# A half unit's low part in one VectorE instruction of 1024 columns instead of two of 512

## The chip, the core and the metric

The kernel runs on one core of a Trainium2 chip. The core has a matrix engine, TensorE (PE, with its weight loads shown apart as PEld), and three engines for elementwise work: VectorE (DVE), ScalarE (ACT) and GpSimd (POOL). SyncE (SP) issues most of the DMA transfers from HBM. SBUF is the on-chip memory that the engines read and write, PSUM the memory that matmuls accumulate into. Each engine runs its instructions in one fixed order and waits where an instruction's inputs or buffers aren't ready. The metric is the device time of one execution in microseconds. Three runs of the kernel before gave 2400.18, 2401.51 and 2401.63, a median of 2401.51; the profiled execution, from which all rows below come, took 2397.69.

## The reference

256 rows of width 1024 in float32 go through six layers. The first four are transformer layers (block 1): an attention mixer of one of three kinds, a layer norm, a SwiGLU feed-forward net, a layer norm.

```python
def first_block(x, positions, ln_g, ln_b, ...):
    for i in range(DEPTH):                       # 4
        kind, j = i % N_MIXERS, i // N_MIXERS
        ...                                      # h = mixer_a, mixer_b or mixer_c of x
        x = layer_norm(DN_ALPHA * x + h, ln_g[i, 0], ln_b[i, 0])
        x = layer_norm(DN_ALPHA * x + swiglu(x, w_gate_up[i], w_down[i]), ln_g[i, 1], ln_b[i, 1])
    return x
```

The last two (block 2) project the normed rows with one wide matrix `w_in`, run three branches on the parts (chunked spatial gating, a Mamba-2 state-space mixer, differential attention), gate each branch's projection with a sigmoid, and follow with `w_out` and a feed-forward net with a causal convolution; their norms are RMS norms. Nearly all arithmetic is matmuls of the 256 rows with weight matrices, 381.88 MB of weights and other inputs being read through the hardware DMA queue in one execution.

## The kernel before, in words

**Matmuls of three products.** PE multiplies in a reduced 32-bit format, `fp32r`. To keep float32 accuracy each operand is split in two: a high part, its value rounded to fp32r, and a low part, what the rounding left. `mm3` (L389 to L396) issues three matmuls for each product: rows high x weights high (L394), rows high x weights low (L395), rows low x weights high (L396). A matmul takes 128 rows of the contraction against 512 columns.

**Weights.** `plan` lists all weight units in the order of their use. A unit is loaded as two half units of 128 x 1024 values (two contraction slices of 512 columns for most matrices; one slice of 1024 for those called `rows`; 128 x 64 for the small `dt`). `load` (L367 to L387) makes a half unit ready: a DMA on SP's queue into a buffer `raw` (four of them), the high part `w[:, 0]` by a copy on ACT (L382), and the low part `w[:, 1] = raw - w[:, 0]` by a subtraction (L385). The result is in one of seven buffers `w` (one more in block 1). A buffer `raw` is free for the next DMA when its low part is made. `get` asks for the next half unit one ahead of the one in use (AHEAD = 1), and L394 to L396 wait for the parts that they read. All but 11 of the 728 half units have their low part made on DVE; the 11 in `self.aside` (L1427 to L1431), which follow directly on a change between mixer and feed-forward weights in block 1, on POOL.

**Two row tiles.** The rows are two tiles of 128, t = 0 and 1. Each runs through the layers as its own stream of steps, a Python generator, with tasks of its own (`spawn`, `turn`), and `run` lets the two streams take turns, tile 1 four turns behind (LAG). So while one tile is in a norm, the matmuls of the other can fill PE. The instruction lists that result are ordered once more by a scheduler under the kernel's language, engine by engine, so that independent instructions stand between dependent ones.

**Norms.** `layer_norm` (L521) adds the residual (L526), takes mean and variance (L507, L509), and a reciprocal root by three Newton steps on one column (`rsqrt`: L469, then L473 and L477 three times), and scales the rows (L533, L536). All are DVE instructions, each of which needs the one before. At the end of block 1 the normed rows are multiplied by the next norm's gain (`rms_norm`, L958, `rmsh`) and transposed by PE (L439). In the second block `yt` is a branch output that PE has transposed and ACT (L432) and DVE (L433) split into its parts; `sg` (L1318) is a branch's projection times its gate. `xth`, `xtl`, `fht` and `ho` are parts of split rows, made the same way.

Four further lines of the program set what the prediction speaks of:

```python
BUFS = dict(wr=4, wh=7, wx=1, ...)                     # raw buffers, w buffers
AHEAD = 1
nc.vector.scalar_tensor_tensor(h, h, r, b[:, s], ...)  # L536, needs the third Newton step
e = nc.gpsimd if 2 * i + a in self.aside else nc.vector
```

The functions that the change touches and what calls them:

Of the kernel before, what the change touches and what calls it, by code (L numbers as in the profile page):

```python
# [9 lines left out]
F32 = mybir.dt.float32  # L10
# [72 lines left out]
class Net:  # L83
# [283 lines left out]
    def load(self, i, a):  # L367
        nc = self.nc
        _, (kt, n), parts = self.units[i]
        k = kt // 2  # L370
        raw = self.wr.tile([P, 1024], F32, name="raw")[:, :k * n]
        rv = raw.rearrange("p (k n) -> p k n", n=n)
        for o, m, src in parts:
            nc.sync.dma_start(rv[:, :, o:o + m], src[:, k * a:k * a + k])
        if i == a == 0:
            self.load_x()
        if i < self.units_1 and (2 * i + a) % (BUFS["wh"] + BUFS["wx"]) >= BUFS["wh"]:
            w = self.own("w", [2, 1024], "wx", F32R)
        else:
            w = self.wh.tile([P, 2, 1024], F32R, name="w")  # L380
        m = k * n
        nc.scalar.copy(w[:, 0, :m], raw)  # L382
        e = nc.gpsimd if 2 * i + a in self.aside else nc.vector
        for s in (slice(0, m // 2), slice(m // 2, m)):
            e.tensor_sub(w[:, 1, s], raw[:, s], w[:, 0, s].bitcast(F32))  # L385
        return w[:, :, :k * n].rearrange("p two (k n) -> p two k n", n=n)


# [1096 lines left out]
```

## Time and profile before

| | before |
|---|---|
| median of three runs | 2401.51 us |
| profiled execution | 2397.69 us |
| its span (first to last instruction) | 2395.8 us |
| mean granted clock of PE | 0.999 |
| PE busy | 2358.1 us, 98% |
| DVE busy | 1739.8 us, 73% |
| ACT busy | 1320.2 us, 55% |
| POOL busy | 148.1 us, 6% |
| low parts on DVE (L385) | 942.9 us in 1434 instructions |
| high parts on ACT (L382) | 758.5 us in 728 instructions |

How to read it: busy time is the time in which an engine has an instruction under way, and consecutive records of one engine can overlap a little, since an instruction may start before the one ahead of it has left the engine; so the pace is read from start to start in a timeline, and the sum of records is somewhat above the time they take. A number in square brackets behind a row is idle time of the engine before it, with the instruction that ended it. The trace names a tile without its buffer number.

### The profile page before, as it was taken

How to read it: one execution, taken by the hardware profiler on the slowest of the kernel's cores; microseconds unless marked ns; L12 is line 12 of the kernel's file. 1: busy time of each engine (PE TensorE's matmuls, PEld its weight loads, DVE VectorE, ACT ScalarE, POOL GpSimd, SP SyncE). 2: the span in 40 equal slices, each digit the busy share in tenths (PEclk: the TensorE clock that was granted, in tenths of full speed). 3: DMA queues.
4: the chain of work that ended last, by engine and by line, in shares of the span. 5: the costliest groups of instructions: out<-in, count | busy, mean ns of one | idle time of the engine just before them, and what ended most of it. 6: DMA issues, size and time to landing. Idle time of an engine off the chain costs nothing.

```text
span 2395.8 us, 35093 instructions
## 1 busy us (share of the span) xinstructions
PE 2358.1 (98%) x11720; PEld 1926.0 (80%) x11720; DVE 1739.8 (73%) x4255; ACT 1320.2 (55%) x2182; POOL 148.1 (6%) x428
## 2 busy tenths in 40 slices
PE   8999999999999999999999999999999999999999
PEld 6788878888788788887778878887888788888887
DVE  7755576666755767557775588987877889987876
ACT  6544456555444555444544445744577656545776
POOL 1100000000100001000010000100011201000111
PEclk9999999999999999999999999999999999999999
DMA  6366654444566545665365657567565686575653
GB/s 233 106 189 189 185 167 132 133 132 131 171 189 187 185 132 167 187 188 184 124 182 190 186 140 168 136 147 198 165 194 184 166 187 132 123 213 172 189 184 115
DMA packets 280117, 400.16 MB, mean 167 GB/s; under 512 B 20588, under 2 KB 205098, under 8 KB 279936
## 3 DMA queue, kind: packets, MB, share of 16 engines
q1 hardware_dynamic: 274784, 381.88, 54.8%
q0 software_dynamic: 5152, 16.05, 2.2%
q8 instruction: 92, 1.51, 0.3%
q14 instruction: 89, 0.73, 0.1%
HBM read 396.81 MB, written 1.05 MB: 166 GB/s over the span
## 4 chain that ended last, share of the span: by engine, by line
PE 87%; DVE 8%; DMA 3%; ACT 2%; issue 1%; SPq 0%; ACTq 0%; DVEq 0%
PE pj L394 21%; PE pj L396 21%; PE pj L395 21%; PE tp L439 4%; PE ch L394 4%; PE ch L396 4%; PE ch L395 4%; PE ch L596 3%; PE ch L634 2%; DVE w L385 2%; DMA raw<-in_w_in_dram 2%; PE tp L646 1%; ACT w L382 1%; DMA raw<-in_a_w_qkv_dram 1%; DVE convy L985 1%
## 5 line engine op out<-in xcount | busy, mean ns | idle before, releaser
L385 DVE TENSOR_TENSOR w<-raw,w 128x512 fp32r<-128x512 f32 x1434 | 942.9, 684 | 469.3 <-ACT w L382 468.2
L382 ACT CAST w<-raw 128x1024 fp32r<-128x1024 f32 x728 | 758.5, 1043 | 661.2 <-PE pj L396 370.9
L394 PE MATMUL pj<-w,xth 128*128 128x512 f32 x2048 | 820.4, 401 | 7.1 <-ACT xth L432 6.8
L395 PE MATMUL pj<-w,xth 128*128 128x512 f32 x2048 | 803.3, 393 | 1.1 <-DVE w L385 1.1
L396 PE MATMUL pj<-w,xtl 128*128 128x512 f32 x2048 | 802.4, 393 | 1.8 <-DVE xtl L433 1.8
L394 PEld LDWEIGHTS pj<-w,xth 128*128 128x128 f32 x2048 | 385.5, 188 | 90.8 <-ACT xth L432 12.4
L396 PEld LDWEIGHTS pj<-w,xtl 128*128 128x128 f32 x2048 | 385.0, 188 | 86.4 <-DVE xtl L433 5.0
L395 PEld LDWEIGHTS pj<-w,xth 128*128 128x128 f32 x2048 | 386.0, 188 | 76.8 <-DVE w L385 2.0
L394 PE MATMUL ch<-w,fht 128*128 128x512 f32 x412 | 171.4, 416 | 1.8 <-ACT fht L432 1.8
L396 PE MATMUL ch<-w,fht 128*128 128x512 f32 x412 | 161.4, 392 | 0.0
L395 PE MATMUL ch<-w,fht 128*128 128x512 f32 x412 | 160.9, 391 | 0.0
L985 DVE SCALAR_TENSOR_TENSOR convy<-xc,ffn_cw,convy 128x128 f32<-128x128 f32 x352 | 100.7, 347 | 7.1 <-POOL ffn_hist L976 2.1
L396 PEld LDWEIGHTS ch<-w,fht 128*128 128x128 f32 x412 | 77.3, 188 | 17.9 <-DVE fht L433 1.0
L394 PEld LDWEIGHTS ch<-w,fht 128*128 128x128 f32 x412 | 77.5, 188 | 15.4 <-ACT fht L432 3.9
L395 PEld LDWEIGHTS ch<-w,fht 128*128 128x128 f32 x412 | 77.9, 189 | 11.9
L623 ACT ACTIVATE pexp<-ch,nm 128x128 f32<-128x128 f32 (+1 forms) x192 | 65.6, 421 | 33.8 <-DVE nm L618 24.0
L827 ACT ACTIVATE ffg<-pj 128x256 f32<-128x256 f32 x88 | 33.8, 384 | 86.2 <-PE pj L396 86.2
L982 ACT ACTIVATE convy<-xc,ffn_cw 128x128 f32<-128x128 f32 x176 | 72.8, 484 | 1.4
L634 PEld LDWEIGHTS ch<-v,pt 128*128 128x128 f32 x576 | 70.6, 192 | 2.9
L394 PE MATMUL pj<-w,fht 128*128 128x512 f32 x180 | 71.3, 396 | 0.0
L396 PE MATMUL pj<-w,fht 128*128 128x512 f32 x180 | 70.7, 393 | 0.0
L395 PE MATMUL pj<-w,fht 128*128 128x512 f32 x180 | 70.2, 390 | 0.0
(333 smaller groups left out, 2758.8 us busy)
## 6 DMA issues: line engine op xcount, KB each, us to landing
raw<-in_w_gate_up_dram SPq DMA_DIRECT2D x352, 256.0 KB, 3.2
raw<-in_w_in_dram SPq DMA_DIRECT2D x128, 512.0 KB, 5.1
raw<-in_w_down_dram SPq DMA_DIRECT2D x88, 512.0 KB, 3.6
raw<-in_ffn_w_up_dram SPq DMA_DIRECT2D x176, 256.0 KB, 3.3
raw<-in_b_w_qkv_dram SPq DMA_DIRECT2D x144, 256.0 KB, 3.1
raw<-in_ffn_w_down_dram SPq DMA_DIRECT2D x44, 512.0 KB, 4.4
raw<-in_a_w_qkv_dram SPq DMA_DIRECT2D x24, 512.0 KB, 4.4
raw<-in_c_w_qkv_dram SPq DMA_DIRECT2D x48, 256.0 KB, 3.2
```

Of the source, the lines that this page charges most:

```text
L382: nc.scalar.copy(w[:, 0, :m], raw)
L385: e.tensor_sub(w[:, 1, s], raw[:, s], w[:, 0, s].bitcast(F32))
L394: mm(ps, xh[:, k, :], wh[:, kk, cols], start=start, stop=False)
L395: mm(ps, xh[:, k, :], wl[:, kk, cols], start=False, stop=False)
L396: mm(ps, xl[:, k, :], wh[:, kk, cols], start=False, stop=stop)
L439: self.nc.tensor.transpose(tp[:, b * P:(b + 1) * P], src[:, b * P:(b + 1) * P], self.ident)
L596: nc.tensor.matmul(svs[par][:, a, j * P:(j + 1) * P], q(par, a), k(par, a, j), start=True, stop=True)
L623: nc.scalar.activation(p[:, a, :(t + 1) * P], sv[:, a, :], AF.Exp, bias=n2[:, a:a + 1])
L634: nc.tensor.matmul(o[:, par + 2 * a, :], pts[par][:, a * (t + 1) + j, :], v(j, par + 2 * a), start=j == 0, stop=j == t)
L827: nc.scalar.activation(g, ps[:, :FFC], AF.Silu)
L982: nc.scalar.activation(y[:, a, :], xc[:, a, 4:], AF.Identity, bias=b[:, 0, c:c + 1], scale=w[:, h, c:c + 1])
L985: nc.vector.scalar_tensor_tensor(y[:, a, :], xc[:, a, o:o + P], w[:, j, c:c + 1], y[:, a, :], op0=OP.mult, op1=OP.add)
```

## The change

The loop over two halves of the columns at the end of `load` is replaced by one subtraction over all of them. High part, buffers, DMAs and matmuls are the same. On the engines that is one instruction where there were two, at DVE 717 for 1434, on POOL 11 for 22. Lines after it move up by one (L385 becomes L384, L433 becomes L432, L958 becomes L957).

```diff
         m = k * n
         nc.scalar.copy(w[:, 0, :m], raw)
         e = nc.gpsimd if 2 * i + a in self.aside else nc.vector
-        for s in (slice(0, m // 2), slice(m // 2, m)):
-            e.tensor_sub(w[:, 1, s], raw[:, s], w[:, 0, s].bitcast(F32))
+        e.tensor_sub(w[:, 1, :m], raw, w[:, 0, :m].bitcast(F32))
         return w[:, :, :k * n].rearrange("p two (k n) -> p two k n", n=n)
```

With fewer instructions the scheduler also places others differently. Two places show it. A number behind a tile's name is that of its buffer's allocation; they are counted anew in the changed program, so the same half unit has another number there.

DVE at the end of block 1 before (1402.6 to 1408 us in the trace): the last layer norm of row tile 0 (`x_93`, `rs_y_13266`), with the half units 13442 and 13464 and row tile 1's residual (`x_120`) between its steps.

```order
L477 SCALAR_TENSOR_TENSOR rs_y_13266<-rs_a_13267,rs_y_13266 128x1
L385 TENSOR_TENSOR w_13442<-raw_13440,w_13442 128x512
L473 SCALAR_TENSOR_TENSOR rs_a_13267<-rs_y_13266,bnve_13264 128x1
L385 TENSOR_TENSOR w_13464<-raw_13462,w_13464 128x512
L477 SCALAR_TENSOR_TENSOR rs_y_13266<-rs_a_13267,rs_y_13266 128x1
L526 SCALAR_TENSOR_TENSOR x_120<-x_120,ch_12083 128x512
L473 SCALAR_TENSOR_TENSOR rs_a_13267<-rs_y_13266,bnve_13264 128x1
L526 SCALAR_TENSOR_TENSOR x_120<-x_120,pj_12084 128x512
L477 SCALAR_TENSOR_TENSOR rs_y_13266<-rs_a_13267,rs_y_13266 128x1
L385 TENSOR_TENSOR w_13464<-raw_13462,w_13464 128x512
L536 SCALAR_TENSOR_TENSOR x_93<-x_93,rs_y_13266,lnb_13219 128x512 x2
L958 TENSOR_TENSOR rmsh_13281<-x_93,ng_13279 128x512
```

A fourth half, the first of 13442, stands eight instructions ahead of the second, behind the norm's L509. The same place in the changed program, where 13442 and 13464 are 13023 and 13044, and the two half units after them 13058 and 13093:

```order
L476 SCALAR_TENSOR_TENSOR rs_y_12849<-rs_a_12850,rs_y_12849 128x1
L384 TENSOR_TENSOR w_13044<-raw_13042,w_13044 128x1024
L472 SCALAR_TENSOR_TENSOR rs_a_12850<-rs_y_12849,bnve_12847 128x1
L525 SCALAR_TENSOR_TENSOR x_120<-x_120,ch_11719 128x512
L476 SCALAR_TENSOR_TENSOR rs_y_12849<-rs_a_12850,rs_y_12849 128x1
L525 SCALAR_TENSOR_TENSOR x_120<-x_120,pj_11720 128x512
L472 SCALAR_TENSOR_TENSOR rs_a_12850<-rs_y_12849,bnve_12847 128x1
L384 TENSOR_TENSOR w_13058<-raw_13056,w_13058 128x1024
L476 SCALAR_TENSOR_TENSOR rs_y_12849<-rs_a_12850,rs_y_12849 128x1
L384 TENSOR_TENSOR w_13093<-raw_13091,w_13093 128x1024
L535 SCALAR_TENSOR_TENSOR x_93<-x_93,rs_y_12849,lnb_12804 128x512 x2
L957 TENSOR_TENSOR rmsh_12864<-x_93,ng_12862 128x512
```

Here too a fourth low part, 13023, stands eight instructions ahead of 13044, behind the norm's L508. The chain's own steps and the two L526 are the same; in place of four halves of two half units there are four whole half units.

DVE in the state-space stretch of the first block-2 layer before (1637 to 1646.7 us in the trace), with the splits of `yt`, the low parts of the half units 15717 to 15788, and the gated projection `sg`:

```order
L385 TENSOR_TENSOR w_15717<-raw_15715,w_15717 128x512
L477 SCALAR_TENSOR_TENSOR rssm1_13505<-rs_a_15631,rssm1_13505 128x1
L433 TENSOR_TENSOR yt_15707<-tp_15708,yt_15707 128x512
L385 TENSOR_TENSOR w_15746<-raw_15744,w_15746 128x512 x2
L385 TENSOR_TENSOR w_15764<-raw_15762,w_15764 128x512 x2
L385 TENSOR_TENSOR w_15788<-raw_15786,w_15788 128x512
L433 TENSOR_TENSOR yt_15736<-tp_15737,yt_15736 128x512
L385 TENSOR_TENSOR w_15788<-raw_15786,w_15788 128x512
L1318 SCALAR_TENSOR_TENSOR sg_15727<-sg_15727,pj_15729 128x512
```

The same place in the changed program, where 15746, 15764 and 15788 are 15261, 15278 and 15301, and the two `yt` 15223 and 15251:

```order
L384 TENSOR_TENSOR w_15261<-raw_15259,w_15261 128x1024
L472 SCALAR_TENSOR_TENSOR rs_a_15150<-rssm1_13083,rmsv_15147 128x1
L432 TENSOR_TENSOR yt_15223<-tp_15224,yt_15223 128x512
L476 SCALAR_TENSOR_TENSOR rssm1_13083<-rs_a_15150,rssm1_13083 128x1
L384 TENSOR_TENSOR w_15278<-raw_15276,w_15278 128x1024
L472 SCALAR_TENSOR_TENSOR rs_a_15150<-rssm1_13083,rmsv_15147 128x1
L384 TENSOR_TENSOR w_15301<-raw_15299,w_15301 128x1024
L476 SCALAR_TENSOR_TENSOR rssm1_13083<-rs_a_15150,rssm1_13083 128x1
L432 TENSOR_TENSOR yt_15251<-tp_15252,yt_15251 128x512
L1317 SCALAR_TENSOR_TENSOR sg_15242<-sg_15242,pj_15244 128x512
```

The low part of 15746 moved from behind the first split of `yt` to ahead of it, and that of 15788 stands whole ahead of the second split.

## Rows read from the trace of the kernel before

**Rows 1.** The page: busy time, share of the span and instructions by engine.
```profile
span 2395.8 us, 35093 instructions
...
PE 2358.1 (98%) x11720; PEld 1926.0 (80%) x11720; DVE 1739.8 (73%) x4255; ACT 1320.2 (55%) x2182; POOL 148.1 (6%) x428
```

**Rows 2.** The page's costliest group: count | busy us, mean ns | idle before, releaser.
```profile
L385 DVE TENSOR_TENSOR w<-raw,w 128x512 fp32r<-128x512 f32 x1434 | 942.9, 684 | 469.3 <-ACT w L382 468.2
```

**Rows 3.** PE's waits, whole run: us in total, times, longest.
```profile
PE tp L439 <- DVE rmsh L958: 3.7, 2, 3.5
PE tp L439 <- DVE rs_a L473: 3.3, 2, 2.2
...
PE pj L396 <- DVE xtl L433: 1.8, 5, 0.5
PE pj L394 <- DVE sg L1318: 1.5, 1, 1.5
...
PE pj L395 <- DVE w L385: 1.1, 1, 1.1
```

**Rows 4.** Busy us and instructions by stretch: length, PE, PEld, DVE, ACT, POOL, clock, DMA.
```profile
150.00:290.00 140.00, 140.00 (x633) 114.73 (x632) 77.22 (x138) 61.12 (x83) 2.00 (x8) 1.00 0.60 186
...
1545.00:1650.00 105.00, 101.88 (x525) 83.48 (x524) 93.24 (x228) 51.70 (x74) 3.87 (x8) 1.00 0.65 157
2030.00:2130.00 100.00, 99.53 (x524) 83.00 (x524) 90.93 (x236) 50.90 (x78) 3.33 (x12) 1.00 0.63 147
```

**Rows 5.** DVE's timeline, two places: start, length, instruction, count.
```profile
14.86 3.09 DVE L385 TENSOR_TENSOR w<-raw,w 128x512 fp32r<-128x512 f32 x5
17.87 0.36 DVE L256 TENSOR_SCALAR rtang<-rtiv,posf 128x8 f32<-128x8 f32 x2
...
1620.83 1.17 DVE L1279 TENSOR_TENSOR xs<-xs,sng 128x1024 f32<-128x1024 f32 x1
1621.92 0.21 DVE L946 SCALAR_TENSOR_TENSOR rmsv<-bnmv 128x1 f32<-128x1 f32 x1
```

**Rows 6.** Timeline of DVE and PE at the end of block 1.
```profile
1402.69 0.68 DVE L385 TENSOR_TENSOR w<-raw,w 128x512 fp32r<-128x512 f32 x1
...
1407.51 1.29 DVE L958 TENSOR_TENSOR rmsh<-x,ng 128x512 f32<-128x512 f32 x2
...
1408.34 1.47 PE L439 MATMUL tp<-ident,rmsh 128*128 128x128 f32 x7 [3.47 <-DVE rmsh L958]
```

**Rows 7.** Slices of 1 us behind that, columns as in rows 4.
```profile
1409.00:1410.00 1.00, 1.00 (x5) 0.98 (x6) 1.00 (x3) 0.59 (x1) 0.00 (x0) 0.50 0.93 160
...
1412.00:1413.00 1.00, 1.00 (x5) 0.81 (x4) 1.00 (x4) 0.18 (x1) 0.00 (x0) 0.84 0.00 0
```

**Rows 8.** POOL's low parts by form, and one pair in the timeline.
```profile
L385 POOL TENSOR_TENSOR w<-raw,w 128x512 fp32r<-128x512 f32 x22 | 28.6, 1319 | 556.8 <-ACT w L382 547.0 <-DVE eg L789 9.8
...
923.34 2.60 POOL L385 TENSOR_TENSOR w<-raw,w 128x512 fp32r<-128x512 f32 x2 [1.04 <-ACT w L382]
923.49 1.24 DVE L473 SCALAR_TENSOR_TENSOR rs_a<-rs_y,bnve 128x1 f32<-128x1 f32 x1
...
926.22 0.20 DVE L473 SCALAR_TENSOR_TENSOR rs_a<-rs_y,bnve 128x1 f32<-128x1 f32 x1
926.44 0.41 PE L439 MATMUL tp<-ident,ob 128*128 128x128 f32 x2 [1.09 <-DVE rs_a L473]
```

**Rows 9.** Timeline of PE and ACT in the first state-space stretch.
```profile
1642.50 0.50 PE L395 MATMUL pj<-w,xth 128*128 128x512 f32 x1 [1.08 <-DVE w L385]
1642.96 1.05 ACT L382 CAST w<-raw 128x1024 fp32r<-128x1024 f32 x1 [0.31 <-DMA raw<-in_w_branch_b_dram]
1646.80 0.47 PE L394 MATMUL pj<-w,yt 128*128 128x512 f32 x1 [1.47 <-DVE sg L1318]
```

## Prediction

> **What bounds the kernel now.** I read the page's busy shares first, to see which engine has no room; then the waits of that engine, to see who ends its idle time; then windows of single stages, and last the timelines of the two or three places where VectorE (DVE) ends a wait. TensorE (PE) is busy for 2358.1 of 2395.8 us [rows 1]: 37.7 us are all that any change off PE can give back. DVE is busy 73% of the span, and the instruction that is changed is its largest group, 942.9 us in 1434 pieces [rows 2]. That looks like much, but in the whole run PE waits once for a low part, 1.1 us; the larger waits on DVE are for the layer boundaries: 3.7 us for the normed rows `rmsh`, 3.3 for what follows a reciprocal root (`rs_a`), 1.5 for `sg` [rows 3]. The windows say where a faster DVE could matter at all: in a feed-forward stretch PE has no idle time (140.00 of 140.00 us), in the state-space stretch of the first block-2 layer DVE is busy 93.24 of 105 us and PE idles 3.12, in that of the second PE idles 0.47 [rows 4]. So most of the 717 half units are made beside matmuls that don't wait for them.
>
> **What one instruction costs.** Five halves queued one behind the other start at 14.86 and the next instruction at 17.87: 0.60 us each from start to start, though a record lasts 0.684 [rows 2, 5]. No low part of 1024 columns exists in the trace. The nearest row is a TENSOR_TENSOR of the same engine with two SBUF inputs of 128x1024 (L1279): a record of 1.17, and 1.09 to the next start [rows 5]. So a pair of 1.20 becomes 1.09 (that row, start to start; I take it) or 1.17 (if the next one waits for the record's end). Over DVE's 717 half units that is 78 or 21 us of DVE time less, 3% or 1% of the span, nearly all beside a busy PE. The upper half of the columns comes 0.03 to 0.11 earlier, the lower half 0.49 to 0.57 later, and whatever is queued behind the first half waits as much longer.
>
> The Trainium skill (VectorE: DVE Perf Modes, section on the fixed extra latency of SBUF-source operations) says that each such instruction pays a fixed latency once, and gives (N+151)/0.96 ns for an fp32 tensor_tensor. By it a pair of 2 x 691 ns becomes 1224, a gain of 0.157 us or 113 us in all, and an instruction that stands in a chain grows by 0.53 instead of my 0.49: the sum below would be 0.2 us higher. The trace has the 0.684 of the rule as a record but 0.60 as the pace, so I go by the pace.
>
> **The end of block 1, 1400 to 1408 us: +2.0.** Here DVE runs the last layer norm of row tile 0 as a chain of dependent instructions, and between any two of them one other instruction is filled in. Before, four of the fill-ins of this chain are halves of low parts (the one at 1402.69 is one of them); the chain ends with `rmsh` at 1407.51, and PE, which has nothing else left, starts again at 1408.34 after 3.47 us of idling [rows 6]. The new order has four low parts at such places too, but whole ones: the two half units 13442 and 13464 in four pieces become four half units in one piece each. The order does not fill in half as many, it fills in as many that are nearly twice as long. So `rmsh` comes 4 x 0.49 = 1.96 us later (4 x 0.57 = 2.28 by the longer record), and PE idles as much longer; I take +2.0. Nothing hides it, since PE's queue is empty. It would be nothing only if the chain before 1400 were shorter by as much, which its order doesn't show. The low parts made there ahead of time are missing from the chain of row tile 1 at 1412 to 1421 (four halves, 2.4 us), but PE waits in the whole run for `xtl` only 1.8 us in five waits [rows 3], so I count nothing back; at most 0.8.
> After that wait the granted clock is 0.50 (1.2 of 2.4 GHz) in the slices 1409 to 1412, three of which the first stands here, 0.84 in the next [rows 7]: the matmuls lose about 3 x 0.50 + 0.16 = 1.7 us there. A longer idle time may leave that as it is (0, which I take) or cost it once more (+1.7).
>
> **POOL's half units: +0.4.** At the boundaries of block 1 eleven half units are made by POOL, 22 halves of 1.319 us [rows 8]. While POOL runs such a pair (923.34, 2.60 us), a DVE instruction of one column with two SBUF inputs takes 1.24 us where it takes 0.20 later in the same chain (926.22); PE restarts at 926.44 after 1.09 [rows 8]. In the trace the first such instruction waits out the first half, the next the second half. With one POOL instruction of 2.5 us the first waits for all of it: from 923.49 to about 925.9, and the second then nothing. What comes between the two moves behind the end, 0.1 to 0.25 us. Of the places where this happens, two end a PE wait (the two waits on `rs_a` in rows 3): 0.4 in all. Nothing, if the one POOL instruction is shorter than the pair by that much; 2.4, if at each place it holds a second instruction for 1.2 more.
> The Trainium skill (GPSIMD Engine Reference, Key points) names the cause, SBUF interfaces that GpSimd shares with VectorE, in contention with DVE instructions with two SBUF inputs; the 1.24 against 0.20 agrees. It gives no price for a longer one; by it the whole of 2.4 would be possible, not forced.
>
> **The state-space stretches: -0.8.** At 1642.50 PE waits 1.08 us for a low part: in DVE's order it is queued behind the split of `yt`. In the new order that low part (15746, now 15261) stands ahead of that split, and the one wait on a low part goes. But next is `sg`, for which PE waits 1.47 at 1646.80, and it is queued behind the low part of 15788 (now 15301) in both orders, whose weights are cast only after their DMA (ACT at 1642.96 starts on the DMA's landing) [rows 9]. So I count 1.1 as gained, 0.3 as given back at `sg`. Bounds: all idle time of both stretches goes, 3.12 + 0.47 = 3.6 less; or the lower half, 0.5 later, makes PE wait at four loads of weights more, +2.
>
> **The sum.** 2.0 + 0.4 - 0.8 = +1.6 us on the profiled execution's 2397.69, so 2399.3. The median of the runs shown is 2401.51, 3.8 above that execution; on its scale 2403.1. About 0.2%, 4.8 us, is what a measurement of this kernel can tell from no change: the forecast is no measurable change. With the bounds above the likeliest case reaches from 2397 (-3.6 at the state space, -0.8 at row tile 1, nothing at the chain) to 2407 (the chain with its clock 2.28 + 1.7, POOL 1.5).
>
> **Rivals.**
> Faster: the shorter low parts reach the ends of waits. For it speaks that the four largest waits on DVE sum to 3.7 + 3.3 + 1.5 + 1.1 = 9.6 us [rows 3], each at the end of a DVE queue in which low parts stand, and that each second half, which frees the raw buffer for the next load, comes earlier. Against it speaks that in the largest of them the count of fill-ins stays four. If two thirds of the 9.6 went: -6.4, about 2395. Chance 0.2.
> Slower: longer fill-ins in dependent chains. A chain's next instruction can't start before the fill-in ahead of it ends, and each fill-in is 0.49 to 0.57 longer. Place: every norm that ends a PE wait; price 2 us for four fill-ins; it decides once a chain holds as many fill-ins as before, that is more half units, and PE's queue is empty meanwhile. For it speaks 1400 to 1408, where just that stands in the order; against it that at the other norms the other row tile's matmuls cover most of it (a PE wait of 1.09 and less). With the last chain at 2.28 + 1.7 and two more chains at 2 each: +8, about 2409.5. Chance 0.31.
> The change doesn't do what it says: if one instruction takes 1.20 like the pair, DVE's load is the same and only the order and the later lower half remain: +2 at the chain, the same verdict; it is within the likeliest case. That case, no measurable change, has 0.49.
> The chance of faster by over 0.2% is then 0.2, within 0.2% 0.49, slower 0.31. The range of 8 in 10 is 2394 to 2411: it leaves out the ends beyond either rival's own time.
>
> **What the new profile would show.** The low part on DVE as 128x1024, mean record 1.15 to 1.22 us, some 820 to 870 us in all instead of 942.9, and PE's busy time unchanged. The wait for `rmsh` at the end of block 1 at 5.4 us instead of 3.5: that is the step I rest on most; if it stays at 3.5 or falls, the chain's count of fill-ins was not what set it. No PE wait for a low part at the first state-space stretch, and a wait for `sg` of 1.5 or more. The one-column DVE instruction beside POOL at 2.4 us. The forecast is wrong if PE's idle sum moves from 37.7 by more than 5, above all if waits of L395 on low parts appear, which would say that the lower half was needed at once.

## The result and the profile after

The change makes the kernel slower: 2419.98 us median of five runs (2419.43 to 2423.79) against 2401.51, a ratio of 1.0086 (95% interval 1.0075 to 1.0097), 18.5 us more. The forecast was 2403.1 in a range of 2394 to 2411, so it was wrong. The slower rival came nearest, but its +8 us is less than half of the loss, and its mechanism holds at one place only.

The page of the changed kernel first, busy time by engine, the costliest group and the shares of the chain that ended last. Compare with [rows 1, 2]:

```profile
span 2417.7 us, 33935 instructions
...
PE 2364.1 (98%) x11720; PEld 1933.5 (80%) x11720; DVE 1700.8 (70%) x3538; ACT 1321.7 (55%) x2184; POOL 150.3 (6%) x417
...
PE 87%; DVE 5%; DMA 3%; issue 2%; ACT 2%; POOL 0%; SPq 0%; DVEq 0%; ACTq 0%; POOLq 0%
...
L384 DVE TENSOR_TENSOR w<-raw,w 128x1024 fp32r<-128x1024 f32 (+1 forms) x717 | 872.2, 1217 | 498.0 <-ACT w L382 494.7
```

The instruction itself does what was said: DVE has 717 instead of 1434, 872.2 us instead of 942.9. DVE has less to do and the kernel is slower. PE has 53.6 us outside its busy time (2417.7 - 2364.1), 15.9 more than before, and its busy time has grown by 6.0 though it computes the same. These are two losses, and both stand in the trace. First PE's waits, whole run: us in total, times, longest. Compare with [rows 3].

```profile
PE tp L438 <- DVE rmsh L957: 6.1, 2, 5.3
PE tp L438 <- DVE x L535: 4.6, 3, 1.5
...
PE tp L438 <- DVE rs_a L472: 4.2, 2, 3.2
PE tp L645 <- ACT pt L647: 3.1, 2, 2.8
PE ch L1091 <- DVE ssl L1087: 2.5, 3, 1.5
PE pj L393 <- DVE sg L1317: 2.5, 1, 2.5
...
PE pj L394 <- DVE w L384: 1.5, 1, 1.5
PE ch L1080 <- ACT sscb L1057: 1.4, 1, 1.4
```

Low parts themselves (L394 on `w`) are waited for once, as before. Most of what grew are waits at the end of a chain of dependent DVE instructions. The wait on L535, three times 1.5 us, is new. The largest is the predicted one; here is its chain, DVE and PE at the end of block 1, start and length in us. First three lines of before, to go with [rows 6]:

```profile
1404.48 0.39 PE L396 MATMUL pj<-w,fht 128*128 128x512 f32 x1
...
1404.91 0.69 DVE L526 SCALAR_TENSOR_TENSOR x<-x,pj 128x512 f32<-128x512 f32 x1
...
1405.58 0.69 DVE L385 TENSOR_TENSOR w<-raw,w 128x512 fp32r<-128x512 f32 x1
```

The changed kernel:

```profile
1418.38 1.22 DVE L384 TENSOR_TENSOR w<-raw,w 128x1024 fp32r<-128x1024 f32 x1
...
1420.18 0.40 PE L395 MATMUL pj<-w,fht 128*128 128x512 f32 x1
...
1420.62 0.69 DVE L525 SCALAR_TENSOR_TENSOR x<-x,pj 128x512 f32<-128x512 f32 x1 [0.17 <-PE pj L395]
...
1421.35 1.22 DVE L384 TENSOR_TENSOR w<-raw,w 128x1024 fp32r<-128x1024 f32 x1
...
1422.56 1.22 DVE L384 TENSOR_TENSOR w<-raw,w 128x1024 fp32r<-128x1024 f32 x1
1423.69 1.41 DVE L535 SCALAR_TENSOR_TENSOR x<-x,rs_y,lnb 128x512 f32<-128x512 f32 x2
1425.02 1.28 DVE L957 TENSOR_TENSOR rmsh<-x,ng 128x512 f32<-128x512 f32 x2
...
1425.85 1.94 PE L438 MATMUL tp<-ident,rmsh 128*128 128x128 f32 x8 [5.27 <-DVE rmsh L957]
```

A whole low part takes 1.13 us from start to start (1422.56 to 1423.69) where a half took 0.60, and four of them stand in the chain: PE waits 5.27 instead of 3.47.

Not all four make up that wait. It begins when PE's last matmul ends (1420.18 + 0.40), and the other row tile's residual (L525 on `pj`), which stands in the chain, needs that matmul's result: DVE idles 0.17 us for it and goes on at 1420.62. What stands ahead of it in the chain was done by then. Behind it stand two whole low parts (1421.35 and 1422.56, together 2.26) with a Newton step between them, where one half (0.60) stood behind it before.

The new waits on L535, at the three layer ends before, hang on the same residual, but not on longer low parts. DVE and PE at the first of them, before:

```profile
301.27 1.40 DVE L536 SCALAR_TENSOR_TENSOR x<-x,rs_y,lnb 128x512 f32<-128x512 f32 x2
302.59 0.68 DVE L526 SCALAR_TENSOR_TENSOR x<-x,ch 128x512 f32<-128x512 f32 x1
...
301.72 0.39 PE L396 MATMUL pj<-w,fht 128*128 128x512 f32 x1
302.15 1.29 PE L439 MATMUL tp<-ident,x 128*128 128x128 f32 x8
```

And in the changed kernel:

```profile
305.27 1.21 DVE L384 TENSOR_TENSOR w<-raw,w 128x1024 fp32r<-128x1024 f32 x1
306.40 0.21 DVE L472 SCALAR_TENSOR_TENSOR rs_a<-rs_y,bnve 128x1 f32<-128x1 f32 x1
...
308.35 0.69 DVE L525 SCALAR_TENSOR_TENSOR x<-x,ch 128x512 f32<-128x512 f32 x1
...
309.26 0.69 DVE L525 SCALAR_TENSOR_TENSOR x<-x,pj 128x512 f32<-128x512 f32 x1
309.86 1.41 DVE L535 SCALAR_TENSOR_TENSOR x<-x,rs_y,lnb 128x512 f32<-128x512 f32 x2
...
308.83 0.39 PE L395 MATMUL pj<-w,fht 128*128 128x512 f32 x1
310.75 1.29 PE L438 MATMUL tp<-ident,x 128*128 128x128 f32 x8 [1.53 <-DVE x L535]
```

Before, the four fill-ins of this chain were four halves (298.13, 298.86, 299.99 and 300.67 in that trace), and PE did not wait for its end. Now they are two whole low parts and, in the two slots that became free, the other row tile's residual (L525), which before stood behind the chain (302.59). From the start of the first Newton step to L535 it takes 5.12 us (304.74 to 309.86) instead of 3.67 (297.60 to 301.27). The low parts are not what lengthens it: two whole ones take 2.26 us, the four halves took 2.40. The second residual starts only at 309.26, 0.04 after PE's last matmul has ended (308.83 + 0.39), and L535 behind it. So PE waits here for a chain that itself waits for PE's last matmul, 1.53 or 1.54 us at all three ends.

The wait for `pt` at 73 in the first layer, 2.8 us for 1.6, is another case again. PE before, and in the changed kernel:

```profile
71.67 0.39 PE L396 MATMUL pj<-w,ho 128*128 128x512 f32 x1
73.70 0.44 PE L646 MATMUL tp<-ident,pexp 128*128 128x128 f32 x2 [1.64 <-ACT pt L648]
...
72.59 0.50 PE L395 MATMUL pj<-w,ho 128*128 128x512 f32 x1
75.91 0.69 PE L645 MATMUL tp<-ident,pexp 128*128 128x128 f32 x2 [2.82 <-ACT pt L647]
```

Behind its last attention scores (L596, now L595) PE had five matmuls left, to the one at 71.67, and now has the one at 72.59: some 0.9 us less to cover the chain. No low part runs on DVE from 66.92 to 75.27, so here too the order changed and not a fill-in's length.

The second loss is PE's clock. Slices of 2 us in the changed kernel: length, busy PE, PEld, DVE, ACT, POOL, granted clock, DMA share, GB/s. Compare with [rows 7].

```profile
73.00:75.00 2.00, 0.08 (x1) 0.00 (x0) 2.00 (x11) 1.09 (x3) 0.11 (x1) 1.00 0.00 0
75.00:77.00 2.00, 1.09 (x6) 1.10 (x7) 1.90 (x9) 1.64 (x8) 0.47 (x1) 0.51 0.37 96
77.00:79.00 2.00, 2.00 (x12) 2.00 (x11) 0.34 (x2) 0.53 (x3) 0.00 (x0) 0.50 0.94 230
...
1423.00:1425.00 2.00, 0.00 (x0) 0.00 (x0) 2.00 (x3) 0.00 (x0) 0.00 (x0) 0.58 0.93 162
1425.00:1427.00 2.00, 1.15 (x6) 1.19 (x7) 2.00 (x5) 0.03 (x1) 0.00 (x0) 0.50 1.00 151
1427.00:1429.00 2.00, 2.00 (x7) 1.41 (x6) 2.00 (x6) 1.71 (x3) 0.00 (x0) 0.50 1.03 146
...
624.00:626.00 2.00, 0.77 (x3) 0.61 (x3) 1.97 (x9) 0.07 (x1) 0.00 (x0) 0.65 0.62 213
626.00:628.00 2.00, 1.96 (x5) 1.37 (x5) 2.00 (x4) 1.35 (x2) 0.00 (x0) 0.50 0.30 39
```

In the profile before, the clock was at 0.50 (1.2 GHz) inside the program at one place, 1409 to 1412, behind 3.47 us of waiting. In this one it is there at four places: at 75 (behind a wait of 2.8 us), 113 (behind waits of 0.9 and 1.8), 625 (behind 3.2) and 1423 (behind 5.3), 23.9 us in the clock records instead of 3.4. In 4.4 of these PE waits anyway; the rest runs at half speed and costs (23.9 - 4.4) / 2 = 9.7 us, against 1.7 before.

So the profiled span grew by 21.9: 15.9 us more waiting, as PE's gaps between matmuls sum (45.3 for 29.4), and 8.0 for the clock; that the two make 23.9 shows how exact such a split is, since PE's ends are modelled. The profiled execution of before is 3.8 us below the median and that of the changed kernel 0.6, so the medians lie 18.5 apart and not 21.9. Over all runs that list it the mean granted clock is 0.9983 in 59 runs of before and 0.9947 in nine of the changed kernel: 4.1 and 12.9 us of the time, 8.8 more, of which 2.2 fall in PE's waits if they lie as in this profile. By this estimate the clock is some 6 to 7 of the 18.5 us. Where the loss came about is read by comparing the start of the n-th 512-column matmul in both traces:

| place, time before | lag gained, us | what is there |
|---|---|---|
| to 90 | +4.7 | start; wait 2.8 for `pt`, clock |
| 106 to 113 | +2.7 | POOL's half unit, clock |
| 299, 800, 1121 | +1.4, +1.4, +1.4 | layer ends, L535 |
| 615 | +3.7 | POOL's half unit, `rs_a` 3.2, clock |
| 1125 to 1160 | -0.4 | given back, not followed up |
| 1400 to 1425 | +1.4 | +2.8, then -1.4 |
| 1545 to 1625 | +3.7 | first state-space stretch |
| 1980 to 2080 | +0.9 | second |
| elsewhere | +1.0 | steps of up to 0.6, not followed up |
| 150 to 290 | 0.0 | feed-forward, PE 140.00 of 140.00 us busy |

### The profile page after: what moved, and what is told of

Its sections match the earlier page's. It is cut to its first block, busy times and chain, and to the rows that moved or that the text cites. A ratio compares the mean times of both kernels' runs of the same rounds, so it can differ in the third digit from the quotient of the medians.

```text
span 2417.7 us, 33935 instructions
## 1 busy us (share of the span) xinstructions
PE 2364.1 (98%) x11720; PEld 1933.5 (80%) x11720; DVE 1700.8 (70%) x3538; ACT 1321.7 (55%) x2184; POOL 150.3 (6%) x417
## 4 chain that ended last, share of the span: by engine, by line
PE 87%; DVE 5%; DMA 3%; issue 2%; ACT 2%; POOL 0%; SPq 0%; DVEq 0%; ACTq 0%; POOLq 0%
PE pj L393 21%; PE pj L395 21%; PE pj L394 21%; PE tp L438 4%; PE ch L393 4%; PE ch L395 4%; PE ch L394 4%; PE ch L595 3%; PE ch L633 2%; DMA raw<-in_w_in_dram 2%; DVE w L384 1%; PE tp L645 1%; ACT w L382 1%; DMA raw<-in_a_w_qkv_dram 1%; DVE x L532 0%
## 5 line engine op out<-in xcount | busy, mean ns | idle before, releaser
L384 DVE TENSOR_TENSOR w<-raw,w 128x1024 fp32r<-128x1024 f32 (+1 forms) x717 | 872.2, 1217 | 498.0 <-ACT w L382 494.7
L394 PE MATMUL pj<-w,xth 128*128 128x512 f32 x2048 | 801.5, 392 | 1.6 <-DVE w L384 1.5
L394 PEld LDWEIGHTS pj<-w,xth 128*128 128x128 f32 x2048 | 385.9, 188 | 77.3 <-DVE w L384 2.8
L394 PE MATMUL ch<-w,fht 128*128 128x512 f32 x412 | 160.9, 390 | 0.0
L394 PEld LDWEIGHTS ch<-w,fht 128*128 128x128 f32 x412 | 77.9, 189 | 11.8
L622 ACT ACTIVATE pexp<-ch,nm 128x128 f32<-128x128 f32 (+1 forms) x192 | 65.9, 421 | 37.6 <-DVE nm L617 23.9
L393 PE MATMUL pj<-w,fht 128*128 128x512 f32 x180 | 71.2, 395 | 0.0
L395 PE MATMUL pj<-w,fht 128*128 128x512 f32 x180 | 70.6, 392 | 0.0
L633 PE MATMUL ch<-v,pt 128*128 128x65 f32 x576 | 70.3, 273 | 0.0
```

What stands on the lines that cost most here:

```text
L384: e.tensor_sub(w[:, 1, :m], raw, w[:, 0, :m].bitcast(F32))
L393: mm(ps, xh[:, k, :], wh[:, kk, cols], start=start, stop=False)
L394: mm(ps, xh[:, k, :], wl[:, kk, cols], start=False, stop=False)
L395: mm(ps, xl[:, k, :], wh[:, kk, cols], start=False, stop=stop)
L622: nc.scalar.activation(p[:, a, :(t + 1) * P], sv[:, a, :], AF.Exp, bias=n2[:, a:a + 1])
L633: nc.tensor.matmul(o[:, par + 2 * a, :], pts[par][:, a * (t + 1) + j, :], v(j, par + 2 * a), start=j == 0, stop=j == t)
```

## Experiments

Theory 1: fill-ins that are longer lengthen the dependent DVE chains that PE waits for, and the clock falls behind the longer waits. Theory 2: POOL's whole instructions hold DVE's with two SBUF inputs and make the losses at 112 and 615. A third possibility is that the new order of instructions costs, not their length.

All kernels but one build on the kernel before and differ in how many instructions make a low part; `aside` are POOL's 11 half units, `ff` the feed-forward units. A ratio is to the runs of before on the same chip, with its 95% interval.

**Whose instruction costs?** The order of the other instructions on every engine is the same in pool_whole as before, and in dve_whole as in the changed kernel, so these two part the change cleanly between DVE and POOL.

```diff
-        for s in (slice(0, m // 2), slice(m // 2, m)):
+        parts = 1 if 2 * i + a in self.aside else 2      # pool_whole
+        parts = 2 if 2 * i + a in self.aside else 1      # dve_whole
+        for s in [slice(j * m // parts, (j + 1) * m // parts) for j in range(parts)]:
```

> Only POOL's 11 half units are made by one instruction of 1024 columns; DVE keeps its pairs of 512, and the order of every engine is that of the kernel before. Theory 1 (the loss is DVE's longer fill-ins in dependent chains, and the low clock behind the longer idle times): +0 to +3 us, no low clock at 113 or 625. Theory 2 (a whole POOL instruction holds a DVE instruction with two SBUF inputs for 2.4 us and so makes the losses at 113 and 625): +6 to +8 us, with the low clock at both. If only the new order of instructions costs: 0.

Ratio 1.0003 (0.9993 to 1.0012): no change. In its trace a whole POOL instruction of 2.4 us does hold a DVE instruction, in pool_whole at 610.64 the L534 of 128x512:

```profile
610.39 2.51 POOL L386 TENSOR_TENSOR w<-raw,w 128x1024 fp32r<-128x1024 f32 x1
...
610.64 2.81 DVE L534 SCALAR_TENSOR_TENSOR x<-x,bnmv,lng 128x512 f32<-128x512 f32 x1
```

but the chain behind it ends little later: PE's longest wait on `rs_a` is 2.8 instead of 2.2. Its profile has the low clock behind that wait (3.4 us from 615), which theory 1 had excluded. By the time theory 2 falls for POOL's instructions alone.

> Only DVE's 717 half units are made whole; POOL keeps its pairs; the order of every engine is that of the changed kernel. Theory 1: +15 to +19 us, the low clock at 75, 625 and 1423 as in the changed kernel. Theory 2: +10 to +13 us, no low clock at 113 and 625, that at 75 and 1423 stays. Under both the wait for rmsh stays at 5.3 us.

1.0073 (1.0056 to 1.0090), some 17 us. DVE's whole instructions carry nearly all of it; the waits are those of the changed kernel (`rmsh` 5.3, L537 three times 1.5, `pt` 2.8). The time is theory 1's. But its profile has no low clock at 113 and 625, which was theory 2's mark; the place of the low clock in one profile does not decide between them, since it changes between executions (last section).

> The changed kernel once more, beside the same runs of before as the others: +18 to +20 us. Against dve_whole's +17 that leaves 1 to 3 us for POOL's whole instructions, at 112 and 615.

1.0083 (1.0068 to 1.0098), 19.8 us at the medians: the result again. Against dve_whole the intervals overlap, so POOL's share, 0 to some 4 us, stays open. The traces have it at 112 and 615: one DVE instruction of one column takes 2.36 us at 110.16 beside POOL's whole one (110.15 to 112.51), PE waits 1.8 for the split behind it, and the clock falls (not in the profile of whole_again, which has it at 1665 instead).

**Length or number?** Quarters, thirds, and a single half:

```diff
+        parts = 2 if 2 * i + a in self.aside else 4      # dve_quarters; 3 in thirds
```
```diff
+            parts = [slice(0, m // 2)]                   # half_only, DVE's units of 1024
...
-        mm(ps, xh[:, k, :], wl[:, kk, cols], start=False, stop=False)
+        lk, lc = (0, cols) if wl.shape[1] > 1 else (kk, slice(0, 512))
+        mm(ps, xh[:, k, :], wl[:, lk, lc], start=False, stop=False)
```

> DVE makes only the first 512 columns of each low part (the low part of the other half is left out, and its matmuls read the first half's instead, so PE's work is the same); POOL keeps its pairs. One instruction for each half unit as in the changed kernel, but each as long as before; DVE has some 430 us less to do. If the length of a fill-in is what costs (theory 1): no slower than before, -6 to 0 us, the wait for rmsh at most 3.5 us, no low clock at 75. If the new order or the lone count of instructions costs: slower by 5 us or more though DVE has so much less to do.

0.9977 (0.9968 to 0.9986): 5 us faster than before, with DVE at 1356.4 us busy. One instruction for each half unit costs nothing here when it is as short as before. But DVE also has 383 us less to do and the scheduler's order is another one, so number, load and order are not parted by this run. With 383 us of DVE work gone the kernel gains only 5 us, so the time hangs little on DVE's load as a whole. At the layer ends the residuals stand behind the chain again, and PE waits there 0.4 us at most. At the end of block 1 the residual that needs PE's last matmul is in the chain, no low part stands behind it, and this is the wait:

```profile
1408.33 1.23 PE L444 MATMUL tp<-ident,rmsh 128*128 128x128 f32 x8 [2.80 <-DVE rmsh L963]
```

> DVE makes each low part in four instructions of 256 columns instead of two of 512, POOL keeps its pairs. If the length of a fill-in sets PE's waits at the ends of norm chains (theory 1): the wait for rmsh falls from 3.5 to about 2.5 us, the low clock at 1409 goes, and in all -3 to +1 us, though DVE's busy time grows by 150 to 250 us. If DVE's load sets the time (rival): +5 us and more, with waits of L395 for low parts in the state-space stretches.

1.0077 (1.0062 to 1.0092), as slow as whole ones. By its time this is the rival's outcome (+5 us and more), not theory 1's (-3 to +1). The chain at the end of block 1 in the timeline of dve_quarters:

```profile
1403.19 0.42 DVE L386 TENSOR_TENSOR w<-raw,w 128x256 fp32r<-128x256 f32 x1
1403.53 0.22 DVE L474 SCALAR_TENSOR_TENSOR rs_a<-rs_y,bnve 128x1 f32<-128x1 f32 x1
...
1404.06 0.68 DVE L527 SCALAR_TENSOR_TENSOR x<-x,ch 128x512 f32<-128x512 f32 x1
1404.66 1.41 DVE L537 SCALAR_TENSOR_TENSOR x<-x,rs_y,lnb 128x512 f32<-128x512 f32 x2
...
1406.82 0.90 PE L440 MATMUL tp<-ident,rmsh 128*128 128x128 f32 x5 [1.70 <-DVE rmsh L959]
```

And two of PE's waits in its whole run:

```profile
PE pj L396 <- DVE w L386: 6.8, 9, 1.5
...
PE tp L440 <- DVE stg L567: 4.2, 6, 1.3
```

A fill-in takes 0.34 us from start to start, and the wait for `rmsh` falls to 1.70 with no low clock behind it, as theory 1 had it. But the length of the fill-ins is not shown to be the reason: in this order the residual that needs PE's last matmul is not in the chain, and L537 starts at 1404.66, while PE is busy until 1405.12. The waits of 1.7, 2.8, 3.5 and 5.3 us in dve_quarters, half_only, before and the changed kernel go with what stands behind PE's last matmul: no residual and no low part, the residual alone, the residual and one half, the residual and two whole ones. Low parts are late elsewhere in dve_quarters, in nine waits of 6.8 us, of which six (4.4 us) are in the state-space stretches, where four quarters take 1.36 us of DVE instead of 1.20. That the load makes these waits is argued; the order has changed as well.

> DVE makes each low part in three instructions of 341 or 342 columns, POOL keeps its pairs. Theory 1 with the load as a second cost: the wait for rmsh between the 3.5 us of pairs and the 1.7 of quarters, DVE busy some 60 us more than before, in all 0 to +8 us, so that two instructions lie near the best. If only length counts: -3 us or less.

1.0039 (1.0024 to 1.0054), 9.5 us at the medians, a little over the expected 0 to 8, with both: `rmsh` 2.3, waits on low parts 6.8 us. Of the ways to cut all of DVE's half units, whole, in two, three or four, two is the fastest.

**Which half units?** By the matrices they belong to:

```diff
+        parts = 1 if "ff" in str(self.units[i][0]) and 2 * i + a not in self.aside else 2       # ffn_whole
+        parts = 1 if i < self.units_1 and not "ff" in str(self.units[i][0]) and 2 * i + a not in self.aside else 2
+        parts = 1 if i >= self.units_1 and not "ff" in str(self.units[i][0]) else 2             # mix2_whole
```

> Only the feed-forward half units of both blocks are made whole on DVE; POOL keeps its pairs. In feed-forward stretches PE has no idle time, and the fill-ins of most norm chains are the mixers' weights. Theory 1: -1 to +2 us, 0 in the feed-forward stretches. If DVE's load counts by itself: -5 us, since it falls by some 40 us.

1.0004 (0.9995 to 1.0014): the feed-forward half units, most of all 717, cost and give nothing that can be told from the noise.

> Only the mixers' half units of block 1 are made whole on DVE; POOL keeps its pairs. Theory 1: +7 to +11 us: 1.5 to 1.8 at each of the three layer ends at 300, 800 and 1121 us, where these half units fill in the norm chains, and 2 to 4 in the first layer, with low clock behind 75. The end of block 1 as before: a wait for rmsh of 3.5 us. With the block-2 mixers' +6 that makes up the whole loss; if it is below +4, something other than the classes' own chains is missing.

1.0026 (1.0017 to 1.0036), 6 us, with the three waits of 1.5 on L537 and a wait for `rmsh` of 3.5. A little under the expected 7.

> Only the half units of block 2's mixers (w_in, branches, w_out) are made whole, all on DVE. The order at the end of block 1 is that of the changed kernel: four whole fill-ins. Theory 1: +6 to +8 us in all, 2.7 of them at 1401 to 1408 with 6.8 us of low clock behind, the rest in the state-space stretch of the first block-2 layer (1560 to 1625); nothing before 1400. If whole instructions cost nothing by themselves and block 1 carries the loss: below +2 us.

1.0027 (1.0016 to 1.0038), 6.5 us, with the wait for `rmsh` of 5.3. Its profiled run has the low clock at 76 and 619 as well, where its work is that of before: there the waits of 1.6 and 2.2 us were followed by it in some executions and not in others. That may be a part of the spread between runs of one kernel (2396.8 to 2404.7 for before).

Together the three classes cost 13.7 us by their ratios, dve_whole 17.5; the intervals, each some 2.4 us to either side, don't part the two.

**Ten of 717.** The half units that fill in the four chains at the layer ends, and their complement:

```diff
+        C = (89, 90, 235, 236, 333, 334, 419, 420, 421, 422)
+        parts = 1 if 2 * i + a in C else 2                                  # chains_whole
+        parts = 2 if 2 * i + a in C or 2 * i + a in self.aside else 1       # all_but_chains
```

> Ten half units alone are made whole: those that fill in the norm chains at the three layer ends at 300, 800 and 1121 us and at the end of block 1; the other 707 of DVE stay pairs. Those four chains have the order of the changed kernel, nearly all the rest that of before. Theory 1: +6 to +8 us: 1.5 at each layer end with a PE wait for L536 behind it, and 1.9 at 1408 with a second 3.4 us of low clock. If the loss is spread over all whole instructions: below +1 us, ten of 717.

1.0022 (1.0013 to 1.0031), 5.3 us by ten low parts that are made in one piece; 6 to 8 were expected. PE's waits in chains_whole:

```profile
PE tp L440 <- DVE rmsh L959: 5.5, 2, 5.3
PE tp L440 <- DVE x L537: 4.6, 3, 1.5
...
PE tp L647 <- ACT pt L649: 1.8, 2, 1.6
```

The waits of these four chains are those of the changed kernel, the others those of before. But making the ten whole also changes the order in these chains, and the residual stands in them as in the changed kernel (304.05 here, 0.04 after PE's last matmul has ended). So at the three layer ends the third possibility is what the traces show, an order that follows from the merging, and at the end of block 1 order and length together.

> The complement: all of DVE's half units whole but those ten. The four chains have the order and the halves of before. Theory 1: +8 to +12 us, what dve_whole lost less what chains_whole loses; no PE wait for L536, the wait for rmsh 3.5 us; the rest of the loss at 75 to 90 and in the first state-space stretch. If the loss is spread over all whole instructions: +16 us and more.

1.0044 (1.0027 to 1.0061), 10.6 us, without the waits on L537 and with `rmsh` at 3.5. 5.3 + 10.6 = 15.9 beside dve_whole's 17.5. So a third of the loss is shown to hang on making ten half units whole; the rest is in the first layer and the state-space stretches, where I did not single out half units.

**A version that beats both?** Quarters only in chains:

```diff
+        parts = 4 if 2 * i + a in (18, 19, 89, 90, 170, 235, 236, 268, 333, 334, 354, 419, 420, 421, 422) else 2
```

> As before, but 15 half units that fill in the norm chains at the layer ends and in the first layer are made in four instructions of 256 columns. Theory 1: the wait for rmsh falls from 3.5 to 2.5 us or less with no low clock behind it; -4 to 0 us in all, without the losses of quarters everywhere. If the scheduler's other moves outweigh it: 0 to +4 us.

1.0000 (0.9990 to 1.0009). The wait for `rmsh` fell to 2.8, not to the expected 2.5, and the low clock behind it stayed. As in half_only no low part is left behind the residual that needs PE's last matmul, so still shorter ones could not take more off this wait as long as the residual stands there. No version beat the kernel before by its times but half_only, which leaves work out.

## Why the prediction was wrong, point by point

**What one instruction costs: right.** 1.13 us from start to start against the 1.09 to 1.17 of the row; the record 1.22. DVE's load fell as said and it was worth nothing, as said. The Trainium skill's formula (VectorE: DVE Perf Modes, section on the fixed extra latency of SBUF-source operations) gives 1.224 for the record, which agrees with 1.223; but pairs went at 0.60 and not at its 0.691, so a pair saves 0.07 us and not 0.157.

**The end of block 1, +2.0: right in size, in part by luck.** The wait rose by 1.80 (5.27 for 3.47), and longer fill-ins are in it. But I counted four of them, and three of the four before (1400.10, 1402.69 and 1403.42) ran while PE still had matmuls. What counts stands behind the residual that needs PE's last matmul: one half then, two whole ones now, 2.26 us for 0.60, and a Newton step. One whole low part in place of that one half would have cost some 0.5 (1.13 - 0.60, an estimate); the second came there by the new order. The 0.8 that might come back later did (-1.4 by 1425). Its clock was taken as unchanged; it stays low twice as long, but over a third of that falls in the wait: 2.1 us lost for 1.7. In all_but_chains it stays low as long, 6.8 us, behind a wait of 3.5, so the longer wait is not shown to be the reason.

**"At the other norms the other row tile's matmuls cover most of it": the step that failed.** I looked for other chains among the waits of the kernel before, where a chain that ends just in time leaves no row. Three layer ends had no wait and now have 1.5 us each, and the first layer's wait for `pt` went from 1.6 to 2.8. The cover went because the order changed: at the layer ends the residual of the other row tile, which needs that tile's last matmul, moved into the chain, so that nothing is left on PE while the chain ends; at `pt` four matmuls fewer were left. The slower rival did not name this. Its place was a norm that ends a PE wait, and these three ended none; its price was the length of the fill-ins, and the low parts take less time there than before. The order of the changed kernel, which could be read at all chains, I read at one only, and there without asking which instruction needs PE's last matmul.

**The clock, 0: wrong.** I weighed it only at 1409, where it was low already. Three places that had run at full clock in the profile before were at half of it in the changed kernel's and lost about 3.0 us (at 75), 1.6 (113) and 3.0 (625) by it: 8.0 us more in all between these two executions, some 6 to 7 by the estimate from all runs. That each fell because its own wait grew is not shown: at 615 the low clock follows waits of 2.2 us in chains_whole and mix2_whole and none of 2.6 in dve_whole and ffn_whole.

**POOL, +0.4: open within 0 to 4.** Alone it costs nothing; beside whole DVE instructions the traces have it at 112 and 615 (there 3.2 us of wait, for 2.2 before, 2.6 in dve_whole and 2.8 in pool_whole).

**The state-space stretches, -0.8: wrong in sign.** The wait on the low part at the first `yt` split did go, and the wait at `sg` took it back, 2.47 for 1.47, both as said, though by 1.0 instead of 0.3. Not seen were new waits in the same stretch: for another low part (1.48, at 1640.63; DVE had stood 3.2 us for ACT's `ssz` ahead of it, L1267), for `sscb` (1.4 for 0.4) and for `ssl` (2.5 in all). PE is busy there 99.52 of 105 us instead of 101.88, and 98.37 of 100 instead of 99.53 in the second layer [rows 4]. What each of these hangs on was not singled out.

**A reading of [rows 3].** The four largest waits on DVE by their sums are 3.7, 3.3, 1.8 (`xtl`) and 1.5, not the four that the faster rival added up; its price would have been 0.5 higher by that, which changes nothing.

## What to carry to other kernels

When the bounding engine runs dry and waits for a chain on another engine, find the instruction in that chain that needs its last result: what stands behind it sets the wait, and longer instructions ahead of it cost nothing as long as they are done by then. Merging instructions also moves others, because the slots that become free are filled again. So before merging such fill-ins read the new order at every chain whose end PE needs, also those that end just in time and leave no wait in the old profile, since that is where a new wait arose here, 1.5 us at each of three. And price a longer wait with the clock that may fall behind it: here some 6 to 7 of 18.5 us, by an estimate.

## What was not expected of the hardware

The low clock behind a wait is not the same in each execution. Waits of 1.6 us (at 72 to 76) are followed by 0.50 in three profiles (chains_whole, mix2_whole, ffn_whole) and of 2.2 us (at 615) in two of these (chains_whole, mix2_whole), and both by full clock in that of before. One wait of 1.5 (mix1_whole, 305) is followed by it, while two waits of 2.6 at 617 (dve_whole, ffn_whole) are not. Nor is its length the same: behind the wait of 2.8 at 73 it lasts 6.8 us in the changed kernel's profile and 3.4 in those of whole_again, dve_whole, mix1_whole and all_but_chains. A DVE instruction of 512 columns with two SBUF inputs, too, was held by POOL's, 2.81 us where the L534 ahead of it took 0.74, not only those of one column.
